# Value columns of a delta-rule mixer projected behind keys and queries, gates kept raw for two tiles, residual transposes issued later

## Chip, cores and metric

One core of one Trainium2 chip runs the whole kernel in one launch. The metric is device time in microseconds (us) of one execution; lower is better.

## What is computed

One decoder layer on x (512 tokens x 1024), all in float32. Cut to its order, the reference is:

```python
x = layer_norm(alpha * x + 0.5 * swiglu_ffn(x, ffn1_w13, ffn1_w2), ln1_g, ln1_b)
h = x @ w_in
gq, gk, gv, gz, ga, gb, dq, dk, dv = split(h)      # 512 columns each; ga, gb: 4
q, k, v = split(silu(causal_depthwise_conv(concat(gq, gk, gv), conv_w)))
q, k = l2_normalize(q), l2_normalize(k)            # 4 heads x 128
g, beta = -exp(a_log) * softplus(ga + dt_bias), sigmoid(gb)
y_a = rms_norm(gated_delta_rule(q, k, v, g, beta), norm_w) * silu(gz)
y_b = differential_attention(rotary(dq), rotary(dk), dv)   # 4 heads, two causal softmax maps each
x = layer_norm(alpha * x + concat(y_a, y_b) @ w_out, ln2_g, ln2_b)
ple = sigmoid(x @ ple_gate_w) * (p @ ple_proj_w)
x = layer_norm(alpha * x + 0.5 * swiglu_ffn(x, ffn2_w13, ffn2_w2) + ple, ln3_g, ln3_b)
```

## The kernel before, in words

Tokens stand in four tiles of 128 (index t). Every matrix product of the layer's weights is made of three TensorE products (`mm3`, lines 297 to 299): both operands are split into a high part that keeps the faster format and a low part that is the rest (`split`, lines 159 and 160: a ScalarE cast and a VectorE subtraction). The current activations lie transposed in XH and XL (channels on partitions), the residual itself in RES (tokens on partitions).

**Residual and transposes.** After each block the residual tile is normalised (`norm_natural`, line 302): statistics on VectorE, an inverse root on GpSimd (line 314), the first 768 columns on VectorE, the last 256 on ScalarE and GpSimd (lines 324 to 326). `norm_turn` (line 336) then transposes the tile on TensorE, eight 128x128 transposes into two PSUM banks (line 341), and splits it into XH and XL. The first FFN ends with products for tile after tile (`ffn`, lines 604 to 624); the turn of a tile follows the normalisation of the next one, and tile 3's turn stands in the first block of the mixer. The output projection (`out_gdn`, line 1288) does the same, and tile 3's turn stands among the gate products of the second FFN (line 787).

**The mixer.** First come attention values and decay inputs (`values_and_gates`), then `keys_queries`: eight columns, four heads of keys and four of queries. A column is 24 products over all 512 tokens from one weight unit; behind it `conv` applies the causal convolution (one ScalarE copy, line 895, three VectorE steps, line 897) and a Silu (line 899). `squares` turns a head to token order and sums its squares.

What follows is written by a small planner in the source. `weave` (line 97) holds lanes, each a generator that says what its last piece costs and how long its answer takes; the first lane that is ready issues next. In order of rank the lanes are: the end of the keys, four preparations of the delta rule (`gdn`, one for each tile), `diagonal` (a small triangular inverse with DMAs through DRAM), `chain` (the recurrence over four chunks, line 1197), sixteen attention heads (`attention`, line 1147: scores L1159, softmax, transposes L1172, products with values L1178; from `i` on a head waits for head `i - 2`), then `fill`, the big products that lie between the others, and last the two halves of the output projection. The chain opens when all `gdn` lanes, the values ("v") and the gates ("z") are said to be done; the attention half of the output projection opens when all heads and the gates are.

`fill` before: the attention keys, four token tiles (each 24 products in three cuts, a copy on ScalarE, line 1013, rotary on GpSimd, lines 906 to 910, and a turn of the tile, line 1002, held back until two cuts of the next tile are issued; the last key tile turns at once); the attention queries in the same way; four value columns of the delta rule with their convolution and `v_turn` (line 1049: four transposes and one VectorE product into VV, line 1052); and four gate tiles, each a Silu on ScalarE (line 1045) and a product with the norm weight on GpSimd (line 1046) into ZG, which lies on MP's first half.

The source gives the order by rank only. When the program is built, the instructions of each engine are put in order by rank and by the times at which their data are expected, so a piece can run before or behind its place in the source. `issue_after` ties a few by hand.

**Buffers.** PSUM has three tags: "a" with three banks (turns, preparation, chain), "b" with two (all big products, key and value turns), "c" with three (attention; two of them for the scores of one head from tile 2 on). "tb" in SBUF has two buffers (convolution, rotary, gates before). Weights come in units of 512 KB through SP's DMA queue into three raw buffers, are split into four pairs of buffers, and are fetched by `ahead`, once for each unit that is used up; a block over token tiles takes four units at once, a column takes one.

The steps that the prediction follows are in these lines:

```python
natural(t, cuts, gbt)                    # ffn, 618
...
if turn and t:                           # 623
    turn(t - 1)
...
if word == "k":                          # fill, 1018
    turn(*last)
    yield 0.5, 0
```

Of the kernel before, what the change touches and what calls it, by code (L numbers as in the profile page):

```python
# [11 lines left out]
AF = mybir.ActivationFunctionType  # L12
# [101 lines left out]
class Layer:  # L114
# [303 lines left out]
    def ffn(self, first_f, rec0, groups, plain, evac_first, ln, natural, turn):  # L418
# [191 lines left out]
        for t in range(NT):  # L610
            cuts = [0, 512, 1024]
            for j in range(t < 2, 2):
                end = not turn and t == NT - 1 and j == 1
                with self.behind([] if t else ended):
                    second(last, t, j, [(0, 256), (256, 512)] if end else [(0, 512)])
                if end:
                    cuts = [0, 512, 768, 1024]
            natural(t, cuts, gbt)
            if turn and t < 2:
                with self.behind(ended):  # L620
                    self.ahead()
                    self.ahead()
            if turn and t:
                turn(t - 1)


    def first_ffn(self):
# [114 lines left out]
    def second_ffn(self):  # L742
        tc, nc = self.tc, self.nc
        act, dve = nc.scalar, nc.vector
        with ExitStack() as zone:
            self.open_sums(zone)
            with ExitStack() as z2:
                pp = z2.enter_context(tc.tile_pool(name="ple", bufs=1))
                PH = pp.tile([P, 2, S], F32R, name="PH")
                PL = pp.tile([P, 2, S], F32R, name="PL")  # L750
                SG = pp.tile([P, NT, D], F32, name="SG")
                pr = [pp.tile([P, S], F32, name=f"pr{k}") for k in range(2)]
                hold = [pp.tile([P, 2, HALF], F32, name=f"hold{k}") for k in range(2)]
                for k in range(2):
                    nc.sync.dma_start(pr[k], self.pT[k])
                sums = self.combine(hold)

                def gate(t, j, wg):
                    tk = slice(t * P, (t + 1) * P)
                    pg = self.ps("b")  # L760
                    for k in range(KT):
                        c = (k % 2) * 512
                        self.mm3(pg, self.XH[:, k, tk], self.XL[:, k, tk], wg[k // 2][0][:, c:c + 512],
                                 wg[k // 2][1][:, c:c + 512], k == 0, k == KT - 1)
                        if t == NT - 1 and k % 2:
                            self.ahead()
                    act.activation(SG[:, t, j * 512:(j + 1) * 512], pg, AF.Sigmoid)

                def project(t, j):
                    tk = slice(t * P, (t + 1) * P)  # L770
                    pj = self.ps("c")
                    for k in range(2):
                        self.mm3(pj, PH[:, k, tk], PL[:, k, tk], wp[k][0][:, j * 512:(j + 1) * 512],
                                 wp[k][1][:, j * 512:(j + 1) * 512], k == 0, k == 1)
                    sg = SG[:, t, j * 512:(j + 1) * 512]
                    dve.tensor_tensor(sg, sg, pj, ALU.mult)
                    rj = self.RES[t][:, j * 512:(j + 1) * 512]
                    dve.scalar_tensor_tensor(rj, rj, ALPHA, sg, ALU.mult, ALU.add)

                wg = [self.take() for _ in range(4)]  # L780
                for t in range(NT):
                    if t == 1:
                        for k in range(2):
                            self.split(PH[:, k, :], PL[:, k, :], pr[k])
                        wp = [self.side(pp, f"wp{k}") for k in range(2)]
                    if t == 2:
                        self.norm_turn(NT - 1)
                    gate(t, 0, wg)
                for _ in range(2):
                    next(sums)  # L790
                wg = [self.take() for _ in range(4)]
                for t in range(NT):
                    gate(t, 1, wg)
                    project(t, 0)
                    for _ in range(2):
                        next(sums, None)
                for _ in sums:
                    pass
                for i in range(2):
                    self.split(*self.quarter(1, 0, 2 * i, 2), hold[i])  # L800
                for t in range(NT):
                    self.ahead()
                    project(t, 1)
                    self.ahead()

            def first(rj, pd, t, j):
                dve.scalar_tensor_tensor(rj, rj, 2.0, pd, ALU.mult, ALU.add)  # L807

            def store(t, lo, hi, rj):
                nc.sync.dma_start(self.out[t * P:(t + 1) * P, lo:hi], rj)  # L810

            def natural(t, cuts, gbt):
                self.norm_natural(t, 4.0 * LN_EPS, gbt, store, 768 if t < NT - 1 else D, cuts)

            self.open_ffn(zone)
            self.ffn(NF, NF - PLAIN, GROUPS2, None, first, G_LN3, natural, None)
# [6 lines left out]
    def mix_zone(self, zone):  # L823
# [88 lines left out]
        def values_and_gates():  # L912
            w = [self.take() for _ in range(4)]
            for t in range(NT):
                if t == 2:
                    self.norm_turn(NT - 1)
                tk = slice(t * P, (t + 1) * P)
                for i, (lo, hi) in enumerate(((0, DVA), (DVA, WIDE // 2))):
                    pq = ps("b")[:, 0:hi - lo]
# [38 lines left out]
        def keys_queries():  # L958
# [11 lines left out]
            for i in range(2):  # L970
                for h in range(H):
# [7 lines left out]
                    if i == 0 and h == 0:  # L979
                        gates()  # L980
                    elif i == 1 and h == 1:
                        gates_decay()
            yield
            squares(*held)
            pool.memset(UU, 0.0)
            dve.tensor_scalar(q1, SSK, RMS_EPS, None, ALU.add)
            dve.tensor_scalar(SSQ, SSQ, RMS_EPS, RMS_EPS * P, ALU.add, ALU.mult)
            dve.reciprocal(q2, q1)
            dve.tensor_tensor(CC, BETA, q2, ALU.mult)
            dve.tensor_tensor(CKR, CC, EG[:, 1], ALU.mult)  # L990
            dve.tensor_scalar(NEG_EG, EG[:, 0], -1.0, None, ALU.mult)
            for c in range(NC):
                pool.tensor_tensor(NRM[:, c], q1[:, c], phalf[:, 0:H], ALU.pow)

        def fill():
            for dst, word in ((DKT, "k"), (DQT, "q")):
                w = [self.take() for _ in range(4)]
                held = None

                def turn(t, d):  # L1000
                    pt = ps("b")
                    turn4(pt, v4(d))
                    dve.tensor_copy(dst[:, :, t * P:(t + 1) * P], v4(pt))
                    said.add((word, t))
                for t in range(NT):
                    pq = ps("b")
# [5 lines left out]
                    d = tb()  # L1012
                    act.copy(d, pq)
                    rotary(d, t)
                    held = (t, d)
                yield 0, 0
                last = held
                if word == "k":
                    turn(*last)
                    yield 0.5, 0  # L1020
            held = last
            for h in range(H):
                pq = ps("b")
                w = self.take()
                for i, (k0, k1) in enumerate(CUTS):
                    columns(pq, w, k0, k1)
                    yield 0.65 * (k1 - k0), 0
                    if i == 1 and h == 0:
                        turn(*held)
                    elif i == 1:  # L1030
                        self.v_turn(*held)
                vt = tb()
                conv(8 + h, pq, v4(vt))
                held = (h, vt)
            w = [self.take() for _ in range(4)]
            for t in range(NT):
                pq = ps("b")
                for i, (k0, k1) in enumerate(CUTS):
                    block(t, w, pq, k0, k1)
                    yield 0.65 * (k1 - k0), 0  # L1040
                    if t == 0 and i == 1:
                        self.v_turn(*held)
                        said.add("v")
                z = tb()
                act.activation(z, pq, AF.Silu)
                pool.tensor_tensor(ZG[:, t], v4(z), bc(VEC[:, V_NW:V_NW + P], 1, H), ALU.mult)
            said.add("z")

        def v_turn(h, vt):
            pt = ps("b")  # L1050
            turn4(pt, v4(vt))
            dve.tensor_tensor(VV[:, :, h, :], v4(pt), bc(NRM[:, :, h], 2, P), ALU.mult)

        self.v_turn = v_turn


        def lv4(l):
# [201 lines left out]
            yield 0.5, 1.0  # L1259


        def project_out(w, half, t):
            tk = slice(t * P, (t + 1) * P)
            for j in range(2):
                pd = ps("b")
                for k in range(4):
                    kk = k + 4 * (1 - half)
# [20 lines left out]
        def out_gdn():  # L1288
# [3 lines left out]
            for t in range(NT):  # L1292
                while ("mix", t) not in said:
                    yield 0, 0.5
                yield from project_out(w, 1, t)
                self.norm_natural(t, LN_EPS, gbt)
                if t:
                    self.norm_turn(t - 1)


        values_and_gates()
# [46 lines left out]
def layout(i):  # L1348
# [30 lines left out]
    wd = np.concatenate([dv[:, :256], ab, dv[:, 256:]], axis=1).reshape(4, 2, P, WIDE // 2).transpose(0, 2, 1, 3)  # L1379
    col_units(gk)  # L1380
    col_units(gq)
    nat_units(dk)
    nat_units(dq)
    col_units(gv)
    nat_units(gz)
    wo = i["w_out"][0]
    for k in (4, 5, 6, 7, 0, 1, 2, 3):
# [38 lines left out]
```

## Time and profile before

| | |
|---|---|
| median of 3 runs | 1098.65 us (1098.52 to 1100.03) |
| the profiled execution | 1099.23 us, its span 1097.4 us |
| TensorE (PE) busy | 1068.6 us, 97% of the span |
| VectorE (DVE) busy | 828.2 us, 75% |
| ScalarE (ACT) busy | 489.9 us, 45% |
| GpSimd (POOL) busy | 112.9 us, 10% |
| weights fetched | 127 units of 512 KB, 88 of 256 KB, 4 of 520 KB |

Times of the trace are us from the start of the span. The busy time of a matrix product overlaps that of the next one, so the time that a product costs is read from start to start. In a row of instructions the number in square brackets is the engine's idle time before it and what ended it. PEld is TensorE's load of the stationary operand.

### The profile page before, as it was taken

How to read it: one execution, taken by the hardware profiler on the slowest of the kernel's cores; microseconds unless marked ns; L12 is line 12 of the kernel's file. 1: busy time of each engine (PE TensorE's matmuls, PEld its weight loads, DVE VectorE, ACT ScalarE, POOL GpSimd, SP SyncE). 2: the span in 40 equal slices, each digit the busy share in tenths (PEclk: the TensorE clock that was granted, in tenths of full speed). 3: DMA queues.
4: the chain of work that ended last, by engine and by line, in shares of the span. 5: the costliest groups of instructions: out<-in, count | busy, mean ns of one | idle time of the engine just before them, and what ended most of it. 6: DMA issues, size and time to landing. Idle time of an engine off the chain costs nothing.

```text
span 1097.4 us, 17374 instructions
## 1 busy us (share of the span) xinstructions
PE 1068.6 (97%) x6627; PEld 939.8 (86%) x6627; DVE 828.2 (75%) x1446; ACT 489.9 (45%) x948; POOL 112.9 (10%) x175
## 2 busy tenths in 40 slices
PE   9999999999999989999999999999999999999996
PEld 7889898989897978778865887779899998999895
DVE  5989796979678366356665658889989696979568
ACT  5745353535333356324365533545544353535231
POOL 1100000000002202432112213100000000000003
PEclk9999999999999999999999999999999999999999
DMA  8633332433242042123210201524343332433212
GB/s 293 202 110 116 103 109 77 117 107 104 77 136 77 1 135 80 36 78 87 58 39 20 77 16 62 163 87 135 101 131 97 106 106 78 118 112 97 77 39 96
DMA packets 44275, 106.03 MB, mean 97 GB/s; under 512 B 10848, under 2 KB 12528, under 8 KB 44192
## 3 DMA queue, kind: packets, MB, share of 16 engines
q1 hardware_dynamic: 37968, 96.71, 29.0%
q0 software_dynamic: 1808, 6.04, 1.7%
q10 hardware_dynamic: 4416, 2.16, 0.7%
q8 instruction: 52, 0.85, 0.3%
q14 instruction: 31, 0.25, 0.1%
HBM read 102.41 MB, written 2.49 MB: 96 GB/s over the span
## 4 chain that ended last, share of the span: by engine, by line
PE 55%; DVE 5%; POOL 2%; DMA 2%; ACT 2%; issue 1%; DVEq 0%; SPq 0%; ACTq 0%; POOLq 0%
PE pb L297 9%; PE pb L298 9%; PE pb L299 9%; PE pc L298 4%; PE pc L299 4%; PE pc L297 4%; PE pa L299 3%; PE pa L298 3%; PE pa L297 3%; PE pc L1159 2%; DMA raw<-in_wa_dram 2%; DVE wl L160 2%; ACT wh L159 1%; PE pa L1092 1%; PE pc L1178 1%
## 5 line engine op out<-in xcount | busy, mean ns | idle before, releaser
L160 DVE TENSOR_TENSOR wl<-raw,wh 128x1024 fp32r<-128x1024 f32 (+3 forms) x137 | 144.2, 1058 | 37.6 <-ACT wh L159 36.4
L159 ACT CAST wh<-raw 128x1024 fp32r<-128x1024 f32 (+3 forms) x137 | 123.2, 906 | 96.7 <-PE pa L298 30.7
L297 PE MATMUL pb<-wh,hh 128*128 128x512 f32 (+1 forms) x356 | 138.3, 389 | 3.7 <-DVE RES L807 1.5
L298 PE MATMUL pb<-wl,hh 128*128 128x512 f32 (+1 forms) x356 | 138.1, 388 | 0.0
L299 PE MATMUL pb<-wh,hl 128*128 128x512 f32 (+1 forms) x356 | 137.8, 387 | 0.0
L229 ACT CAST th<-tr 128x512 fp32r<-128x512 f32 x160 | 98.7, 620 | 83.4 <-PE pc L298 48.2
L233 DVE TENSOR_TENSOR tl<-tr,th 128x512 fp32r<-128x512 f32 x160 | 109.7, 687 | 11.0 <-ACT th L229 10.2
L190 ACT CAST wh<-raw 128x512 fp32r<-128x512 f32 x88 | 54.6, 623 | 135.1 <-PE pb L299 90.8
L297 PE MATMUL pb<-wh,XH 128*128 128x512 f32 (+2 forms) x288 | 110.8, 385 | 2.2 <-ACT wh L159 0.6
L298 PE MATMUL pb<-wl,XH 128*128 128x512 f32 (+2 forms) x288 | 106.1, 369 | 1.0 <-DVE wl L160 0.9
L299 PE MATMUL pb<-wh,XL 128*128 128x512 f32 (+2 forms) x288 | 105.9, 368 | 0.0
L298 PE MATMUL pa<-XL,wh 128*128 128x256 f32 (+1 forms) x344 | 100.0, 291 | 0.2 <-DVE XL L160 0.2
L297 PE MATMUL pa<-XH,wh 128*128 128x256 f32 (+1 forms) x344 | 100.0, 291 | 0.2 <-ACT wh L159 0.2
L299 PE MATMUL pa<-XH,wl 128*128 128x256 f32 (+1 forms) x344 | 99.9, 290 | 0.0
L297 PE MATMUL pc<-XH,th 128*128 128x256 f32 x320 | 90.6, 283 | 0.0
L298 PE MATMUL pc<-XL,th 128*128 128x256 f32 x320 | 90.6, 283 | 0.0
L299 PE MATMUL pc<-XH,tl 128*128 128x256 f32 x320 | 90.6, 283 | 0.0
L490 DVE TENSOR_TENSOR RES<-RES,pb 128x512 f32<-128x512 f32 (+1 forms) x81 | 54.6, 677 | 45.1 <-PE pb L299 44.4
L191 DVE TENSOR_TENSOR wl<-raw,wh 128x512 fp32r<-128x512 f32 x88 | 60.2, 691 | 32.2 <-ACT wh L190 32.0
L297 PEld LDWEIGHTS pb<-wh,hh 128*128 128x128 f32 x356 | 66.9, 188 | 19.4 <-DVE RES L807 1.8
L299 PEld LDWEIGHTS pb<-wh,hl 128*128 128x128 f32 x356 | 66.9, 188 | 13.7
L298 PEld LDWEIGHTS pb<-wl,hh 128*128 128x128 f32 x356 | 66.9, 188 | 13.2 <-DVE wl L191 0.3
(303 smaller groups left out, 2639.8 us busy)
## 6 DMA issues: line engine op xcount, KB each, us to landing
raw<-in_wa_dram SPq DMA_DIRECT2D x127, 512.0 KB, 3.7
raw<-in_wb_dram SPq DMA_DIRECT2D x88, 256.0 KB, 2.7
raw<-in_wd_dram SPq DMA_DIRECT2D x4, 520.0 KB, 3.7
RES<-in_xn_dram POOLq DMA_DIRECT2D x4, 512.0 KB, 6.3
gb<-in_gb_dram POOLq DMA_DIRECT2D x8, 256.0 KB, 3.9
xr<-in_xT_dram ACTq DMA_DIRECT2D x7, 256.0 KB, 4.4
out_dram<-RES SPq DMA_DIRECT2D x5, 256.0 KB, 2.1
TT<-in_gb_dram POOLq DMA_DIRECT2D x4, 256.0 KB, 3.6
```

What stands on the lines that cost most here:

```text
L159: return (self.nc.scalar.copy(hi, src), self.nc.vector.tensor_tensor(lo, src, hi.bitcast(F32), ALU.subtract))
L160: self.nc.vector.tensor_tensor(lo, src, hi.bitcast(F32), ALU.subtract))
L190: nc.scalar.copy(hi, r)
L191: nc.vector.tensor_tensor(lo, r, hi.bitcast(F32), ALU.subtract)
L229: act.copy(h, t)
L233: dve.tensor_tensor(hl[1], t, hl[0].bitcast(F32), ALU.subtract)
L297: pe.matmul(o, wh, xh, start=first, stop=False)
L298: pe.matmul(o, wh, xl, start=False, stop=False)
L299: pe.matmul(o, wl, xh, start=False, stop=last)
L490: dve.tensor_tensor(rj, rj, pd, ALU.add)
L1092: pe.matmul(pt[:, h * P:(h + 1) * P], MP[:, 0, c, h, :], TT[:, c, h, :], start=True, stop=True)
L1159: pe.matmul(sc[m], DQT[r, h, t * P:(t + 1) * P], DKT[r, h, 0:n], start=True, stop=False)
```

## The change

Five things. The four value columns leave `fill` and stand in `keys_queries` behind the queries, one column at a time without a cut; the norm factors NRM that `v_turn` needs are worked out at the first of them. The last key tile's turn is held back into the first query tile, and the last query tile's into the first gate tile. A gate tile is copied raw into ZG by ScalarE, and after every second one a Silu and the GpSimd product run over both. In the first FFN the turns of tiles 0 and 1 are issued behind the second half of tile 2's products and the first half of tile 3's, those of tiles 2 and 3 ahead of the second and third block of `values_and_gates`; at the output projection likewise, with tiles 2 and 3 turned behind the first and second gate block. The units of gv stand ahead of dk's in DRAM, as they are now used.

```diff
@@ ffn
                 if end:
                     cuts = [0, 512, 768, 1024]
+                if turn and (t, j) in ((2, 1), (3, 0)):
+                    turn(t - 2)
             natural(t, cuts, gbt)
...
-            if turn and t:
-                turn(t - 1)
@@ second_ffn
-                    if t == 2:
-                        self.norm_turn(NT - 1)
                     gate(t, 0, wg)
+                    if t < 2:
+                        self.norm_turn(NT - 2 + t)
@@ values_and_gates
-                if t == 2:
-                    self.norm_turn(NT - 1)
+                if t in (1, 2):
+                    self.norm_turn(NT - 3 + t)
@@ keys_queries
+            for h in range(H):
+                pq = ps("b")
+                columns(pq, self.take(), 0, KT)
+                if h == 0:
+                    squares(*held)
+                    dve.tensor_scalar(q1, SSK, RMS_EPS, None, ALU.add)
+                    for c in range(NC):
+                        pool.tensor_tensor(NRM[:, c], q1[:, c], phalf[:, 0:H], ALU.pow)
+                else:
+                    v_turn(*held)
+                vt = tb()
+                conv(8 + h, pq, v4(vt))
+                held = (h, vt)
             yield
-            squares(*held)
+            v_turn(*held)
+            said.add("v")
             pool.memset(UU, 0.0)
-            dve.tensor_scalar(q1, SSK, RMS_EPS, None, ALU.add)
...
-            for c in range(NC):
-                pool.tensor_tensor(NRM[:, c], q1[:, c], phalf[:, 0:H], ALU.pow)
@@ fill
-            for dst, word in ((DKT, "k"), (DQT, "q")):
+            held = None
+            for word in "kq":
                 w = [self.take() for _ in range(4)]
-                held = None
...
-                    held = (t, d)
+                    held = (word, t, d)
                 yield 0, 0
-                last = held
-                if word == "k":
-                    turn(*last)
-                    yield 0.5, 0
-            held = last
-            for h in range(H):
-                pq = ps("b")
-                w = self.take()
-                for i, (k0, k1) in enumerate(CUTS):
-                    columns(pq, w, k0, k1)
-                    yield 0.65 * (k1 - k0), 0
-                    if i == 1 and h == 0:
-                        turn(*held)
-                    elif i == 1:
-                        self.v_turn(*held)
-                vt = tb()
-                conv(8 + h, pq, v4(vt))
-                held = (h, vt)
             w = [self.take() for _ in range(4)]
...
                     if t == 0 and i == 1:
-                        self.v_turn(*held)
-                        said.add("v")
-                z = tb()
-                act.activation(z, pq, AF.Silu)
-                pool.tensor_tensor(ZG[:, t], v4(z), bc(VEC[:, V_NW:V_NW + P], 1, H), ALU.mult)
+                        turn(*held)
+                act.copy(ZG[:, t], v4(pq))
+                if t % 2:
+                    z = ZG[:, t - 1:t + 1].rearrange("p t h b -> p (t h) b")
+                    act.activation(z, z, AF.Silu)
+                    pool.tensor_tensor(z, z, bc(VEC[:, V_NW:V_NW + P], 1, 2 * H), ALU.mult)
@@ out_gdn
-                yield from project_out(w, 1, t)
+                for j in range(2):
+                    yield from project_out(w, 1, t, (j,))
+                    if j == 0 and t > 1:
+                        self.norm_turn(t - 2)
                 self.norm_natural(t, LN_EPS, gbt)
-                if t:
-                    self.norm_turn(t - 1)
@@ layout
     col_units(gk)
     col_units(gq)
+    col_units(gv)
     nat_units(dk)
     nat_units(dq)
-    col_units(gv)
     nat_units(gz)
```

## Rows read from the trace of the kernel before

**Rows 1.** The profile page, part 1: TensorE's busy time, share, instructions.

```profile
PE 1068.6 (97%) x6627; PEld 939.8 (86%) x6627; DVE 828.2 (75%) x1446; ACT 489.9 (45%) x948; POOL 112.9 (10%) x175
```

**Rows 2.** Waits of TensorE, whole span: us in total, times, longest us.

```profile
PE pa L341 <- POOL RES L326: 3.6, 4, 1.3
```

**Rows 3.** TensorE's timeline at the end of the first FFN: start us, us, engine.

```profile
346.76 0.82 PE L341 MATMUL pa<-CST,RES 128*128 128x128 f32 x6
...
349.05 0.48 PE L299 MATMUL pb<-wh,hl 128*128 128x512 f32 x1
...
352.35 1.17 PE L341 MATMUL pa<-CST,RES 128*128 128x128 f32 x8
353.27 0.48 PE L298 MATMUL pb<-wl,hh 128*128 128x512 f32 x1
...
357.25 0.82 PE L341 MATMUL pa<-CST,RES 128*128 128x128 f32 x6
...
359.51 0.37 PE L297 MATMUL pb<-wh,XH 128*128 128x264 f32 x1
...
365.32 0.27 PE L341 MATMUL pa<-CST,RES 128*128 128x128 f32 x1
```

**Rows 4.** The timeline of all engines there: GpSimd's last piece of tile 0.

```profile
348.08 0.72 POOL L326 TENSOR_TENSOR RES<-RES,gb 128x256 f32<-128x256 f32 x1
```

**Rows 5.** TensorE's timeline behind the output projection: turns of tiles 0 and 2.

```profile
670.34 0.81 PE L341 MATMUL pa<-CST,RES 128*128 128x128 f32 x6
...
671.90 0.48 PE L297 MATMUL pb<-wh,XH 128*128 128x512 f32 x1
...
683.87 0.82 PE L341 MATMUL pa<-CST,RES 128*128 128x128 f32 x6
...
685.40 0.48 PE L297 MATMUL pb<-wh,XH 128*128 128x512 f32 x1
686.29 0.50 PE L298 MATMUL pb<-wl,XH 128*128 128x512 f32 x1 [0.41 <-DVE wl L160]
```

**Rows 6.** TensorE's timeline at the end of the attention keys.

```profile
468.62 1.89 PE L1074 MATMUL pa<-KQ 128*128 128x256 f32 x8
472.09 0.66 PE L871 MATMUL pb<-CST,tb 128*128 128x128 f32 x4 [1.59 <-POOL tb L910]
```

**Rows 7.** The timeline at one of the two waits for a value turn.

```profile
558.64 0.60 PE L871 MATMUL pb<-CST,tb 128*128 128x128 f32 x4
...
559.32 0.38 PE L1220 MATMUL pa<-VV,UU 128*128 128x128 f32 x2
...
560.03 0.50 PE L297 MATMUL pb<-XH,wh 128*128 128x512 f32 x1 [0.33 <-DVE VV L1052]
```

**Rows 8.** ScalarE's groups, 380 to 700 us: count | busy us, mean ns | idle.

```profile
L899 ACT ACT_TABLE_LOAD x6 | 7.7, 1283 | 6.2 <-DVE tb L897 6.2
L1164 ACT ACT_TABLE_LOAD x5 | 6.4, 1283 | 4.3 <-DVE amx L1162 4.3
```

**Rows 9.** Timelines of GpSimd, VectorE and TensorE at one gate tile.

```profile
582.06 1.27 POOL L1046 TENSOR_TENSOR MP<-tb,VEC 128x512 f32<-128x512 f32 x1 [5.39 <-ACT tb L1045]
...
582.09 1.25 DVE L1184 SCALAR_TENSOR_TENSOR aso<-aso 128x1 f32<-128x1 f32 x1
...
584.42 0.94 PE L1178 MATMUL pc<-DV,tt 128*128 128x128 f32 x6 [0.56 <-DVE DQT L1186]
```

**Rows 10.** Windows: stretch, length, busy us of PE, PEld, DVE, ACT, POOL; clock.

```profile
541.00:615.00 74.00, 71.95 (x338) 48.84 (x337) 45.19 (x105) 46.19 (x95) 12.02 (x22) 1.00 0.12 35
615.00:656.20 41.20, 40.35 (x259) 35.89 (x257) 24.11 (x50) 17.59 (x53) 7.80 (x7) 1.00 0.15 41
```

**Rows 11.** TensorE's groups: two of 541 to 615, one of 615 to 656.2.

```profile
L297 PE MATMUL pb<-wh,XH 128*128 128x512 f32 x32 | 13.4, 420 | 0.3 <-DVE VV L1052 0.3
...
L297 PE MATMUL pb<-XH,wh 128*128 128x512 f32 x24 | 10.0, 418 | 0.3 <-DVE VV L1052 0.3
...
L297 PE MATMUL pb<-wh,XH 128*128 128x512 f32 x33 | 13.7, 415 | 0.0
```

More of the change, by code (lines that the diff above doesn't have):

```diff
@@ L991, in keys_queries, with turn @@
             dve.tensor_scalar(NEG_EG, EG[:, 0], -1.0, None, ALU.mult)
-            for c in range(NC):
-                pool.tensor_tensor(NRM[:, c], q1[:, c], phalf[:, 0:H], ALU.pow)
         def fill():
-            for dst, word in ((DKT, "k"), (DQT, "q")):
+            held = None
+            for word in "kq":
                 w = [self.take() for _ in range(4)]
-                held = None
-                def turn(t, d):
+                def turn(word, t, d):
                     pt = ps("b")
                     turn4(pt, v4(d))
-                    dve.tensor_copy(dst[:, :, t * P:(t + 1) * P], v4(pt))
+                    dve.tensor_copy((DKT if word == "k" else DQT)[:, :, t * P:(t + 1) * P], v4(pt))
                     said.add((word, t))
@@ L1052, in v_turn @@
             dve.tensor_tensor(VV[:, :, h, :], v4(pt), bc(NRM[:, :, h], 2, P), ALU.mult)
-        self.v_turn = v_turn
         def lv4(l):
@@ L1259, in chain, with project_out @@
             yield 0.5, 1.0
-        def project_out(w, half, t):
+        def project_out(w, half, t, js=(0, 1)):
             tk = slice(t * P, (t + 1) * P)
-            for j in range(2):
+            for j in js:
                 pd = ps("b")
```

## The prediction

> **What bounds the kernel now.** I read four views in this order. The table of engines [rows 1] says that TensorE is busy 97% of the span, so all that an edit of order can win is what TensorE waits, plus the time in which a product is held up inside a busy stretch. The list of waits of TensorE, longest first, names who ended them; its longest line is the transposes of the normed residual, which wait four times for GpSimd's last piece of the normalisation [rows 2]. The timeline of TensorE around each such place gives the size of a wait from start to start of its products, which is firmer than the busy column. The windows of the two mixer stretches [rows 10] show what covers the latency of the attention heads and of the chain, the point where this change can lose. The granted clock is 1.00 in both, so no term below is a change of clock.
>
> The profiled execution took 1099.23 us (a span of 1097.4 and 1.8 around it), 0.6 us above the median of the runs shown, 1098.65. I sum against 1099.2 and take the same difference off the median. A difference under 0.2%, 2.2 us, is about what a measurement of this kernel can't tell from no change.
>
> **The change part by part.**
>
> *Transposes behind the first FFN.* An undisturbed turn (eight transposes) takes 353.27 - 352.35 = 0.92 us. The turn of tile 0 takes 349.05 - 346.76 = 2.29 and that of tile 2 359.51 - 357.25 = 2.26 [rows 3], so 1.37 + 1.34 = 2.7 us are waits. By the program, the turn of tile 0 now stands behind both products of tile 2's halves. In the trace it ran 7 products before the end of those. Fourteen products lie between 349.05 and 352.35, 0.23 us each, so it starts 1.6 us later, at 348.4. Its first six transposes last until 349.1, and GpSimd's last piece is ready at 348.08 + 0.72 = 348.8 [rows 4]: no wait is left. The turn of tile 2 moves behind the whole first block of values (359.51 to 365.32, 5.8 us), long after its data. What needs it, values of tile 2, comes one block later still. I take **-2.7 us**; the bounds are -2.7 and 0.
>
> *Transposes behind the output projection.* The first turn takes 671.90 - 670.34 = 1.56, 0.64 too much. The third takes 685.40 - 683.87 = 1.53, but the gate block behind it waits for the low half of its weights anyway: its second product starts at 686.29, 0.66 later than it would [rows 5]. Today the transposes cover part of that wait; taken away, the wait grows by what they used, up to 0.92, and the transposes still come later. So -0.64 at one place against a loss of about that at the other: **0**, bounds -1.2 and +0.9.
>
> *The last key turn.* It is held over into the first query tile, behind two thirds of that block. Today TensorE stands 1.59 us for GpSimd's rotary at the end of the keys [rows 6]; counted from the end of the eight products before it, it is 1.7. Eighteen query products now lie between, 4 us of cover for a wait of 1.7. The attention heads that need all keys come much later. **-1.7**, bounds -1.7 and 0. The last query turn moves from the first value column to the first gate tile in the same way: 0.
>
> *Value columns out of the fill, behind the queries.* Ninety-six products of 0.23 us, 21.8 us, move and cost the same. In the fill, the transposes of a finished value head make the next column wait for their PSUM bank; this was seen twice, 0.33 us each [rows 7], and goes: **-0.7**. In the new place the same turn stands three times between two columns, with both banks of that tag in use: from the last transpose of 558.64 to the next column at 560.03 the trace has about 1.0 us that is not column work. Three of them are +3.0 if nothing comes between; the lower bound is 0, because the delta-rule preparation, several microseconds of products on other banks, depends on nothing that is still missing. That such a thing is drawn forward is seen in the same rows: a product of the chain (L1220), which the program has behind the end of the gates, ran at 559.32. I take **+1.0**, nearer the lower end. ScalarE's table loads between Silu and Exp, 11 in these two lines at 1.28 us [rows 8], fall by about 7, 9 us of ScalarE; TensorE hardly waits for that engine there, so 0 (bound -1).
>
> *Gate weights.* The four units of the gates are now fetched and split during one query tile instead of one with each value column. A block that takes four fresh units at its start waited 0.66 in [rows 5]; heads can stand in between, so **+0.5**, bounds 0 and +1.4.
>
> *Raw gates.* Four Silu and four GpSimd products over 512 columns become four copies, and two of each over 1024. On ScalarE that is some more work under cover. On GpSimd a product of 1.27 us becomes one of about 2.5. While one ran, a VectorE instruction on a single column, begun 0.03 us later, took 1.25 us, and TensorE waited 0.56 for what hung on it [rows 9]. Taken with the next part. The Trainium skill (SBUF — State Buffer, section Terms, the line on the shared port pair) says that VectorE and GpSimd hold that pair exclusively for a full instruction, the loser blocking fully; the rows agree so far. By that rule alone one wait would grow by some 1.3 us and the sum with it; by the row, in which less than half of the block reached TensorE, by about 0.6.
>
> *What covers the heads and the chain.* Between 541 and 615 us, 56 x 3 = 168 big products (38 us) of values and gates alternate with the heads' 36 us; between 615 and 656, 33 x 3 products of the output projection (22 us) fill the chain, and TensorE is idle 0.85 us in 41 [rows 10, 11]. After the change the value products are gone from the first stretch (72 of the 168), and most of the first gate tile comes ahead of it: some 18 us of fill are left, the gates end before half of the heads' work is done, and the chain starts beside them. Heads and chain then cover each other, the output projection behind both. About 18 us of heads stand against 22 us of gaps, so idle time of 4 us is the plain reading, up to 8 if both wait together, 0 if output projection blocks are drawn forward as L1220 was. A gain is possible too, up to 2 us, from a lighter VectorE and ScalarE. With the GpSimd block I take **+0.6**, bounds -2 and +8.
>
> **Sum**: -2.7 - 1.7 - 0.7 + 1.0 + 0.5 + 0.6 = -3.0 us. 1099.2 - 3.0 = 1096.2 in a profiled run like this one; against the median **1095.6 us**.
>
> **Rivals.**
> *Chain and heads uncovered (slower).* The place is the stretch from the end of the gates to the end of the last head. For it: 21.8 us of cover leave, and the heads have started no earlier in their own order; each needs many small steps on three engines. Against it: the forward draw of rows 7. At 7 us of idle time instead of 0.6 the sum is +3.4, 1102.0 us. It decides from 0.6 + 3.0 + 2.2 = 5.8 us on. Chance 0.23.
> *Waits exchanged.* The value turns cost their full 3.0 and the late stretch 3: -5.1 + 3.0 + 0.5 + 3 = +1.4, 1100.0 us. For it: the column stage has only two banks of this tag. Against it: free preparation work. Chance 0.15.
> *The change doesn't do what it says.* The order on TensorE isn't the program's: the turn of tile 0 stands behind 48 products of its group in the program and ran behind 65. If the turns are again put where their data seem ready, 2.7 stays and the sum is -0.3, 1098.4 us. Against it: a place later in the program is a lower rank. Chance 0.10.
>
> **How the numbers follow.** My forecast, several waits removed and the cover kept, has 0.52; it is faster by over 0.2%. The exchange and the unchanged order give the same time, 0.25. The uncovered stretch gives slower, 0.23. All gains with no cost are -5.1 - 2 - 1 = -8.1, 1090.5; for the top I take the slow rival with another microsecond, 1103. The forecast's own range is 1091 to 1096.4.
>
> **What would show it.** Right: the list of waits has the residual's transposes for GpSimd at under 1 us; the turn of the last keys waits for nothing; no wait for the value turns in the stretch of the heads; table loads down by about seven. Wrong: TensorE idle over 4 us between the end of the gates and the output projection, with waits on the heads' or the chain's VectorE and ScalarE steps; columns that wait a microsecond each for the value turns; a gate block behind the output projection that waits over 1.5 us for its weights.

## The result and the profile after

The changed kernel takes **1106.17 us** (median of 11 runs, 1102.45 to 1112.11) beside 1098.65 for the kernel before: ratio 1.0071, 95% interval 1.0051 to 1.0092, so slower by 0.7%. I had forecast 1095.6 and a range up to 1103.0. The execution with the profile took 1102.71 us, a span of 1100.9.

In the table of engines TensorE still stands at 97%, which says nothing of where the time went:

```profile
PE 1070.4 (97%) x6627; PEld 942.6 (86%) x6627; DVE 826.3 (75%) x1446; ACT 486.5 (44%) x947; POOL 111.9 (10%) x173
```

The list of waits of TensorE in the changed kernel (us in total, times, longest) does:

```profile
PE pc L1170 <- ACT tt L1166: 3.8, 2, 3.5
PE pa L1197 <- ACT ST L1225: 2.2, 1, 2.2
...
PE pc L1170 <- DVE DQT L1178: 1.3, 1, 1.3
PE pb L297 <- ACT AB L928: 1.3, 1, 1.3
PE pb L871 <- POOL tb L910: 1.0, 1, 1.0
PE pb L297 <- DVE tb L897: 0.8, 2, 0.6
...
PE pa L341 <- POOL RES L326: 0.4, 1, 0.4
```

The same places in the kernel before, where L1178 is the heads' product that is L1170 now:

```profile
PE pb L297 <- DVE tb L897: 1.8, 2, 1.2
...
PE pb L871 <- POOL tb L910: 1.6, 1, 1.6
...
PE pc L1178 <- DVE DQT L1186: 0.6, 1, 0.6
...
PE pb L297 <- ACT AB L928: 0.4, 1, 0.4
```

The residual's transposes, 3.6 us before [rows 2], now wait 0.4 us. At the head of the list stand two waits that were not there, both for ScalarE: those of the heads' products with values (L1170) and of the chain (L1197). The same heads' products also wait longer for VectorE, 1.3 us for 0.6, and so does the values block behind the first FFN for ScalarE (L928), 1.3 us for 0.4.

Windows of the changed kernel (us, then busy us of PE, PEld, DVE, ACT, POOL with instruction counts, granted clock, DMA share, GB/s):

```profile
340.00:420.00 80.00, 76.30 (x445) 65.62 (x443) 50.68 (x96) 33.23 (x83) 19.63 (x23) 1.00 0.24 73
420.00:541.00 121.00, 119.64 (x592) 94.75 (x591) 67.96 (x153) 52.13 (x120) 34.22 (x61) 1.00 0.26 72
541.00:615.00 74.00, 68.27 (x422) 52.43 (x420) 43.30 (x109) 37.07 (x100) 17.36 (x26) 1.00 0.14 44
615.00:656.20 41.20, 37.04 (x211) 29.16 (x212) 22.41 (x59) 15.96 (x54) 4.78 (x9) 1.00 0.00 1
541.00:660.00 119.00, 109.11 (x648) 84.74 (x647) 66.87 (x169) 53.03 (x153) 22.13 (x35) 1.00 0.09 27
```

The same for the kernel before, where [rows 10] don't have it:

```profile
340.00:420.00 80.00, 74.33 (x434) 63.61 (x434) 48.36 (x94) 32.94 (x82) 16.85 (x20) 1.00 0.21 67
420.00:541.00 121.00, 119.11 (x663) 96.45 (x662) 69.52 (x166) 45.09 (x121) 39.35 (x72) 1.00 0.25 68
541.00:660.00 119.00, 115.56 (x606) 86.81 (x605) 72.36 (x158) 65.25 (x153) 19.82 (x28) 1.00 0.15 44
```

Idle time is window less PE. From 340 to 541 us it falls from 7.6 to 5.1. The residual's transposes and the last key turn have their share in that; 1.0 us of it is the wait for the convolution (L897), which falls as much in `key_only` below, where nothing at that place is changed. In the two mixer windows it rises from 2.05 + 0.85 [rows 10] to 5.73 + 4.16, by 7.0 us. The DMA share of 0.00 in the second is the output projection not fetching weights. In the timeline no product of L297 to L299 runs between 590.3 and 639. The heads begin 20 us later, behind the moved columns (first scores at 504.2 instead of 484.1); the last product of the last head starts at 637.4 instead of 612.2, and the program opens the output projection only behind all heads.

What such a wait is made of, in the timeline of the changed kernel (lines of TensorE and ScalarE, not all of them):

```profile
595.48 1.06 ACT L1039 ACTIVATE MP<-MP 128x1024 f32<-128x1024 f32 x1
595.77 0.66 PE L1222 MATMUL pa<-ta,KD 128*128 128x128 f32 x4
596.84 1.28 ACT L1156 ACT_TABLE_LOAD   x1 [0.29 <-DVE amx L1154]
597.17 0.49 PE L1164 MATMUL pc<-CST,tt 128*128 128x128 f32 x3
598.70 0.55 ACT L1156 ACTIVATE pc<-pc,amx 128x384 f32<-128x384 f32 x1
599.26 0.58 ACT L1225 COPY ST<-pa 128x512 f32<-128x512 f32 x1
599.89 0.94 PE L1197 MATMUL pa<-ST,KQ 128*128 128x128 f32 x6 [2.23 <-ACT ST L1225]
...
630.06 0.60 PE L1164 MATMUL pc<-CST,tt 128*128 128x128 f32 x4
631.35 0.67 ACT L1156 ACTIVATE tt<-pc,amx 128x512 f32<-128x512 f32 x1
632.01 0.65 ACT L1156 ACTIVATE pc<-pc,amx 128x512 f32<-128x512 f32 x1
633.26 0.30 ACT L1239 ACTIVATE VV<-KQ 128x128 f32<-128x128 f32 x1
633.55 0.57 ACT L1166 COPY tt<-pc 128x512 f32<-128x512 f32 x1
634.17 1.16 PE L1170 MATMUL pc<-DV,tt 128*128 128x128 f32 x8 [3.51 <-ACT tt L1166]
```

The transposes end at 630.66, but ScalarE copies them out at 633.55 only: in its queue the softmax of the next head (L1156) and the chain's squares (L1239) stand ahead. In the same way the chain's state is in PSUM at 596.43 and copied at 599.26, behind a table load and a head's softmax. (The table load is the way back from the Silu of a gate pair, L1039. In `tile_gates` below, which has no pairs, this wait isn't in the list, but another one for ScalarE of 2.1 us is.) In these two places the heads and the chain don't cover each other; they queue for one ScalarE.

### The profile page after: what moved, and what is told of

It reads as the page before. It is cut to its first block, busy times and chain, and to the rows that moved or that the text cites. A ratio compares the mean times of both kernels' runs of the same rounds, so it can differ in the third digit from the quotient of the medians.

```text
span 1100.9 us, 17363 instructions
## 1 busy us (share of the span) xinstructions
PE 1070.4 (97%) x6627; PEld 942.6 (86%) x6627; DVE 826.3 (75%) x1446; ACT 486.5 (44%) x947; POOL 111.9 (10%) x173
## 4 chain that ended last, share of the span: by engine, by line
PE 51%; DVE 7%; ACT 3%; DMA 3%; POOL 2%; issue 2%; DVEq 0%; SPq 0%; ACTq 0%; POOLq 0%
PE pb L297 8%; PE pb L298 8%; PE pb L299 8%; PE pc L297 4%; PE pc L299 4%; PE pc L298 4%; PE pa L298 3%; PE pa L299 3%; PE pa L297 3%; DMA raw<-in_wa_dram 2%; PE pc L1151 2%; DVE wl L160 1%; ACT wh L159 1%; PE pa L1084 1%; DVE tb L897 1%
## 5 line engine op out<-in xcount | busy, mean ns | idle before, releaser
L160 DVE TENSOR_TENSOR wl<-raw,wh 128x1024 fp32r<-128x1024 f32 (+3 forms) x137 | 142.2, 1044 | 38.8 <-ACT wh L159 37.8
L297 PE MATMUL pb<-wh,hh 128*128 128x512 f32 (+1 forms) x356 | 138.1, 389 | 2.4 <-ACT wh L159 1.1
L299 PE MATMUL pb<-wh,hl 128*128 128x512 f32 (+1 forms) x356 | 137.8, 387 | 0.0
L297 PE MATMUL pb<-wh,XH 128*128 128x512 f32 (+2 forms) x288 | 109.6, 381 | 2.7 <-ACT AB L928 1.3
L299 PE MATMUL pb<-wh,XL 128*128 128x512 f32 (+2 forms) x288 | 106.0, 368 | 0.0
L297 PE MATMUL pa<-XH,wh 128*128 128x256 f32 (+1 forms) x344 | 100.3, 292 | 0.0
L299 PE MATMUL pa<-XH,wl 128*128 128x256 f32 (+1 forms) x344 | 100.1, 291 | 0.0
L297 PE MATMUL pc<-XH,th 128*128 128x256 f32 x320 | 90.6, 283 | 0.0
L299 PE MATMUL pc<-XH,tl 128*128 128x256 f32 x320 | 90.6, 283 | 0.0
L297 PEld LDWEIGHTS pb<-wh,hh 128*128 128x128 f32 x356 | 66.9, 188 | 17.3 <-ACT wh L159 1.5
L299 PEld LDWEIGHTS pb<-wh,hl 128*128 128x128 f32 x356 | 66.9, 188 | 13.7
```

The lines of the kernel that those rows point to most:

```text
L160: self.nc.vector.tensor_tensor(lo, src, hi.bitcast(F32), ALU.subtract))
L297: pe.matmul(o, wh, xh, start=first, stop=False)
L299: pe.matmul(o, wl, xh, start=False, stop=last)
```

## The experiments

The kernel before ran beside each group; its medians were 1096.8 to 1097.5 us. The diffs are against the kernel named, cut to the core.

**One part alone, and one part undone.** `v_only` is before with nothing but the columns moved; `v_back` is the changed kernel with only the columns back in the fill; `turns_only` and `key_only` are before with one kind of turn moved.

```diff
 v_only (before)                         v_back is its reverse, on the changed kernel
+            for h in range(H):
+                pq = ps("b")
+                columns(pq, self.take(), 0, KT)
...
 key_only (before)
-                if word == "k":
-                    turn(*last)
-                    yield 0.5, 0
...
 turns_only (before)
+                if turn and (t, j) in ((2, 1), (3, 0)):
+                    turn(t - 2)
...
-            if turn and t:
-                turn(t - 1)
...
```

> The kernel before with one part of the change: the value columns behind keys and queries; turns, gates and the last key turn as before. Theory (cover): the loss comes from this part, since heads and chain then run without big products beside them. Expected 1105 to 1110 us, as far above the changed kernel as the changed kernel's other parts save (2 to 4 us), a spread between runs of several us, and a mean granted clock under 0.997 in the slower runs. Rival (gates): the loss comes from the gate pairs, whose long GpSimd products hold VectorE up; then 1097 to 1099.5 us with the small spread of the kernel before.

> The changed kernel with the value columns back in the fill, all else as changed. Cover: 1094 to 1097 us (the turns give 2.7, the last key turn some 1 to 2), spread of the kernel before, granted clock 0.998 in all runs, TensorE idle under 4 us between the end of the delta-rule levels and the output projection. Gates: above 1100 us.

> The kernel before with the residual turns alone moved. Both theories: 1095.5 to 1097 us (the waits of 1.4 and 1.3 us behind the first FFN gone, nothing net at the output projection). Second rival (exchange): a new wait behind the turns takes the gain, 1098 to 1099.5 us.

> The kernel before with nothing but the last key and query turn of a tile held back behind the next block. If the trace of the changed kernel reads rightly (2.7 us less issue time around the key turn), 1095 to 1096.5 us. If holding the turn costs something later (the query's products are late for the heads), 1098 us or more.

Measured: `v_only` 1104.52 us, ratio 1.0058 (1.0044 to 1.0072); `v_back` 1094.66, 0.9969 (0.9959 to 0.9980); `turns_only` 1095.00, 0.9976 (0.9967 to 0.9985); `key_only` 1094.01, 0.9972 (0.9963 to 0.9981). The loss is in the place of the columns; all that is left without it is a gain. The changed kernel and `v_back` differ by that place alone, and by 1.0071 / 0.9969 = 1.010, some 11 us. Moved alone, from the kernel before, the columns cost 7.0 us: the price depends on what else is changed.

**How much cover.** `v_half` leaves two of the four column groups in the fill.

```diff
 v_half (changed kernel)
-            for h in range(H):
+            for h in range(2):
...
+            for h in range(2, H):
...
```

> The changed kernel with two of the four groups of value columns projected behind the queries, and two left in the fill beside the heads. The cover theory: the time lies between the kernel with all columns back in the fill (2.8 us below before) and the changed kernel (8 to 10 us above before), that is 1097 to 1103 us, the last head's output ends near 624 us, between 611 and 637 to 643, and the granted clock falls for less time than in the changed kernel. If what costs is that columns leave the fill at all (their place behind the queries), half of them cost half in the stretch before 541 us, and not between 590 and 640.

Measured 1098.12 us, 1.0019 (1.0010 to 1.0028): between the two, as cover would have it. The last product of its last head starts at 626.4, also between (610.9 in `v_back`). The window 541 to 660 has 6.8 us idle, against 9.9 in the changed kernel and 4.0 in `v_back`; from 420 to 541 it has 0.8 us against 0.7 in `v_back`, so half of the columns cost nothing behind the queries that would show (first `v_half`, then `v_back`):

```profile
541.00:660.00 119.00, 112.19 (x608) 83.67 (x606) 68.56 (x168) 59.01 (x157) 20.45 (x33) 1.00 0.10 32
```

```profile
541.00:660.00 119.00, 115.00 (x607) 87.42 (x607) 72.58 (x159) 65.95 (x159) 18.02 (x28) 1.00 0.15 45
```

**Other cover: a miss.** `out_early` opens the attention half of the output projection tile by tile, to put big products beside the heads.

```diff
 out_early (changed kernel)
+                while not {("attn", t, h) for h in range(H)} <= said:
+                    yield 0, 0.5
...
-        need_out = {("attn",) + th for th in heads} | {"z"}
+        need_out = {"z"}
...
```

> The changed kernel with the attention half of the output projection opened tile by tile, as soon as a tile's heads and the gates are done, instead of after all heads. Cover: its 192 big products go between heads and chain, TensorE's idle time in the stretch from 555 to 640 us falls from 9.9 us to under 4, granted clock 0.997 or more in all runs, 1094 to 1098 us. Gates or exchange: the time stays at 1102 to 1106 us, since nothing of either is touched.

Measured 1107.2 us, 1.0084 (1.0070 to 1.0098): no help. The first of its blocks ran at 600.2, between the heads, and the last head's last product moved from 637.4 to 656.7. By the program the blocks' turns share the heads' PSUM tag; that this held the heads up is argued, not shown. The idle time, 4.8 us from 600 to 640 and none from 640 to 660 in the changed kernel, moved with the heads:

```profile
600.00:640.00 40.00, 38.30 (x234) 30.16 (x234) 24.81 (x69) 17.09 (x65) 7.84 (x12) 1.00 0.00 1
640.00:660.00 20.00, 14.70 (x68) 10.75 (x67) 9.37 (x27) 7.51 (x25) 2.50 (x5) 0.91 0.00 0
```

**Relief of the heads with the columns still moved.** `heads_first` ranks the heads ahead of the chain, `heads_b` gives them the gates' PSUM banks once the gates are done, `heads_both` does both.

```diff
 heads_first (changed kernel): the line of chain() below the heads' lanes
-        lanes.append(Lane(chain(), lambda: need_chain <= said))
...
+        lanes.append(Lane(chain(), lambda: need_chain <= said))
 heads_b (changed kernel)
-            pt = ps("c")
+            spare = "b" if "z" in said else "c"
+            pt = ps(spare)
...
-            po = ps("c")
+            po = ps(spare)
```

> The changed kernel with the heads ranked ahead of the chain. Heads: the last head ends some 5 us earlier and the chain later, in part under the output projection, which covers it as in the kernel before: 1098 to 1103 us. Cover: heads without the chain beside them wait more, the chain follows, and the sum is the same or worse: 1102 to 1112 us.

> The changed kernel with the transposes and the output of each head issued after the gates in the two banks of tag b, which stand empty there, instead of sharing the three banks of tag c with the scores. Theory (heads): the sixteen heads are a series of about 130 us whose pace their banks and steps set, and the change starts them 20 us later; so with more banks the last head ends 6 us or more ahead of 637 us and the kernel takes 1096 to 1101 us. Rival (cover): only big products beside heads and chain help; then the last head ends where it did and the time stays at 1102 to 1110 us.

> The changed kernel with the heads ahead of the chain of the first output tile, and with their transposes and outputs in the gates' PSUM banks once the gates are done. If the two reliefs add (each took 5 to 8 us off the changed kernel), 1096 to 1099 us. If both only remove the same waits, 1099.5 to 1101 us as each alone. Idle of TensorE between 541 and 660 us: 4 us or less in the first case, about 6.5 in the second.

Measured: `heads_first` 1100.88 us, 1.0042 (1.0027 to 1.0056); `heads_b` 1100.56, 1.0034 (1.0022 to 1.0047), though the last head's last product came only 0.7 us earlier (636.7), not the 6 us expected; `heads_both` 1095.44, 0.9990 (0.9981 to 0.9998). Against the changed kernel beside them (`after_again` below, 1.0088) the two reliefs add, and with the columns still moved they give back 9 us against the first measurement of the changed kernel, 11 against the second. In the list of waits of `heads_both` neither the 3.5 nor the 2.2 us for ScalarE is left. Its window has 4.6 us idle:

```profile
541.00:660.00 119.00, 114.45 (x679) 89.00 (x678) 71.01 (x174) 56.72 (x158) 22.14 (x35) 1.00 0.11 34
```

**The control.** `back_heads` has both reliefs and the columns in the fill (the diffs of `v_back` and `heads_both` together).

> The changed kernel with the value columns back in the fill (2.8 to 3.4 us below before) and with both reliefs of the heads (their rank ahead of the chain, the gates' PSUM banks). With the columns moved, the two reliefs took 12 us off. If what they relieve is only there because the heads stand alone, they are worth little beside a fill that covers them: 1092.5 to 1095 us, at most 2 us from the same kernel without them. If they are simply better for the heads, whatever stands beside them, 1087 us or less, and the columns would cost what they cost in either form.

Measured 1094.14 us, 0.9979 (0.9969 to 0.9988), against 0.9969 without the reliefs: worth nothing there. So what they relieve exists only when the heads stand without cover. Read the other way, the place of the columns costs 11 us without the reliefs and about 1 with them (0.9990 against 0.9979).

**The changed kernel once more**, without an edit, as `after_again`.

> The changed kernel again, for comparison on this chip. 1102 to 1110 us; runs with a lower mean granted clock are the longer ones, by about 11 us for each hundredth, and a profile with a clock of 0.996 or less shows the half clock inside the stretch of heads and chain.

Measured 1108.21 us, 1.0088 (1.0065 to 1.0111). Its profiled execution took 1109.12 us, 6.4 more than the first one. The list of waits from 541 to 660 is nearly the same, and so is the idle time, 10.1 us against 9.9. The granted clock is not:

```profile
541.00:660.00 119.00, 108.92 (x617) 85.43 (x616) 67.17 (x166) 53.10 (x153) 22.13 (x35) 0.93 0.09 27
...
560.00:575.00 15.00, 13.56 (x67) 9.15 (x66) 7.83 (x23) 5.98 (x15) 4.69 (x7) 1.00 0.06 19
575.00:579.00 4.00, 4.00 (x12) 2.39 (x12) 1.08 (x5) 2.89 (x7) 0.74 (x2) 0.58 0.00 0
...
596.00:599.50 3.50, 3.50 (x17) 3.20 (x16) 3.07 (x3) 0.98 (x1) 2.35 (x1) 0.51 0.10 39
...
637.00:644.00 7.00, 5.91 (x27) 5.69 (x28) 3.46 (x11) 2.71 (x10) 1.72 (x3) 0.51 0.01 2
```

0.5 is the lower of the two levels, 1.2 GHz. The program got 617 products done in the window instead of 648, and the last product of the last head starts at 643.4 instead of 637.4.

**Gates.** `tile_gates` and `both_tile` are the changed kernel and `heads_both` with the gates made one tile at a time again. `turns_key` is before with both kinds of turns: `v_back` without the paired gates.

```diff
 tile_gates, both_tile (changed kernel, heads_both)
-                act.copy(ZG[:, t], v4(pq))
-                if t % 2:
...
+                z = tb()
+                act.activation(z, pq, AF.Silu)
...
```

> The changed kernel with the gates tile by tile as before (Silu and a 512-column GpSimd product for each), the columns still moved. If the pairs cost nothing, 1102 to 1110 us, as the changed kernel on this chip within 2 us; the earlier runs add up to 1102 (1104.5 with the columns moved alone, less 2.6 for the turns), so a pair cost of 2 to 4 us, by GpSimd's longer products, would show here as 1101 to 1103 us against 1105 to 1107.

> The kernel before with the residual turns ahead of the last block and with the last key and query turn held back; value columns stay in the fill and gates are made tile by tile. Alone the turns took 2.6 us and the key turn 3.1 us off. If they add, 1091 to 1092 us, and the gate pairs of the changed kernel cost the 2 to 3 us by which the changed kernel with its columns back in the fill (ratio 0.9969) misses that sum. If they do not add, because the heads and the chain give part of an earlier start back, 1094 to 1095 us, and the gate pairs cost nothing here either.

> The changed kernel with both reliefs of the heads (1095.4 us with them) and with the gates made one token tile at a time again. If a paired gate holds up the heads and the chain wherever it falls, as it seems to beside a full fill (3 us between the kernel with both turns and the changed kernel with its columns back), 1092 to 1093.5 us. If it costs something only beside a full fill, as the changed kernel with gates by tile suggests (no difference to the changed kernel), 1095 to 1096 us. What then still separates it from 1090.7 us, the kernel with both turns and the columns in the fill, is the price of the moved columns once the heads are relieved.

Measured: `tile_gates` 1105.81 us, 1.0082 (1.0069 to 1.0095); `both_tile` 1097.59, 1.0002 (0.9990 to 1.0014), no better than with pairs; `turns_key` **1090.74, 0.9942** (0.9930 to 0.9955), the fastest of all and faster than both kernels, where the ratios of the two turns multiply to 0.9948. So beside a full fill the pairs cost about 3 us (0.9969 against 0.9942), and with the columns moved nothing that shows. From 541 to 660 us `turns_key` has 2.1 us idle, `v_back` 4.0, though the profiled execution of `turns_key` was its slowest (1093.42):

```profile
541.00:660.00 119.00, 116.86 (x612) 87.90 (x611) 72.97 (x166) 65.62 (x157) 19.42 (x29) 1.00 0.15 49
```

The timeline of `v_back` has the place, the last pair beside the chain:

```profile
611.95 1.28 ACT L1042 ACT_TABLE_LOAD   x1
613.24 1.06 ACT L1042 ACTIVATE MP<-MP 128x1024 f32<-128x1024 f32 x1
...
614.37 2.36 POOL L1043 TENSOR_TENSOR MP<-MP,VEC 128x1024 f32<-128x1024 f32 x1 [3.90 <-ACT MP L1042]
...
614.77 1.98 DVE L1181 SCALAR_TENSOR_TENSOR aso<-aso 128x1 f32<-128x1 f32 x1
...
615.08 0.50 PE L297 MATMUL pb<-wh,XH 128*128 128x512 f32 x1 [0.94 <-ACT XH L159]
...
617.41 0.66 PE L871 MATMUL pc<-CST,DQT 128*128 128x128 f32 x4 [1.15 <-DVE XL L160]
```

In `turns_key` the same VectorE step is L1179, and it falls behind the gate's product:

```profile
609.62 1.28 POOL L1041 TENSOR_TENSOR MP<-tb,VEC 128x512 f32<-128x512 f32 x1
...
612.99 0.53 DVE L1179 SCALAR_TENSOR_TENSOR aso<-aso 128x1 f32<-128x1 f32 x1
```

In `v_back` a step on one column stands 1.98 us beside the 2.36 us product; the split of the next operand (L160) is queued behind it and TensorE waits 1.15. Ahead of that, 2.3 us of table load and Silu hold up a cast, another 0.94. The Trainium skill (SBUF — State Buffer, section Terms) has the loser of the shared port pair block for the other's whole instruction; the row agrees: the step ends with the product, at 616.7. The 0.53 us in `turns_key` end in the same way, at 613.5, with a GpSimd step of the chain (L1205, 612.46 + 1.04).

**Turns with the columns moved.** `v_turns` is `v_only` with the residual turns of `turns_only`.

> The kernel before with the value columns projected behind keys and queries, and with the two residual turns ahead of their last block; gates are made one token tile at a time and the last key and query turn are done at once. If the parts add, it takes the time of the value columns alone (7.0 us above before in the run of the first call) less the 2.5 us of the turns: 1101 to 1102.5 us beside a before of 1097.2 to 1097.5. If the residual turns are worth nothing once the heads stand alone, 1104 us or more. Neither the held key turn nor the paired gates are in it, so a time of 1105 us or more would clear both of them of what is left of the loss.

Measured 1104.46 us, 1.0067 (1.0049 to 1.0085): the turns' 2.5 us don't show. In its profile the heads start 2.8 us earlier than in `v_only` (507.0 against 509.8) and the span is shorter (1101.4 against 1106.3), but the medians are alike, and the runs spread over 7 us. What swallows the gain was not settled.

## Why the prediction failed

**Failed step: "What covers the heads and the chain".** The step gave the right mechanism and named 4 us of idle time as "the plain reading", but its +0.6 is the share of the GpSimd block alone: the idle time itself went into the sum at nothing, trusting that (in its words) "Heads and chain then cover each other" and that output projection blocks would be drawn forward as one product of the chain had been [rows 7]. None was drawn forward: the program opens that projection behind all heads, and the last head came 25 us later. Where it was forced, in `out_early`, it did not help. And heads and chain held each other up at ScalarE. In place of the 0.6 the two mixer windows lost 7.0 us. The slow rival was priced at that: 7 us of idle time and +3.4. The profiled execution at full clock came out at +3.5 (1102.71 against 1099.23). That the two agree so closely is in part luck: the gain before 541 us was 2.5 us, less than the 3.4 us forecast there, and another 1 us net lies outside these windows, where the sum has no term for it. `v_half`, `heads_both` and `back_heads` show the cause, each from another side.

**Failed too: "no term below is a change of clock".** The rows of before have 1.00 in both mixer windows, and I took that as given. Between the two profiled executions of the changed kernel, with nearly the same waits, the clock is the difference I can see for 6.4 us. The median lies 3.5 us above the profiled run and past the range. Most of that goes with the clock: the five runs with a mean of 0.994 or less took 1107.34 us and more, the six others 1106.17 and less. It isn't all, since the median run itself has 0.997. Why the clock fell in one execution and not in the other is open.

**Residual turns: -2.7 and 0 forecast, -2.6 measured** (`turns_only`). The wait for GpSimd fell from 3.6 to 0.4 us in the changed kernel; the wait at L928 grew by 0.9 us, with the turns alone too, and was not foreseen. In the traces the wait at L897 fell by 1.0 us besides; no run shows that the turns did this, and without it they would have fallen short of the forecast.

**Last key turn: -1.7 forecast, -3.1 measured** (`key_only`). Its own wait fell from 1.6 to 0.4 us. The rest is not at the turn: idle time falls from 5.7 to 4.8 us from 340 to 420, mostly at L897, and from 3.4 to 1.9 from 541 to 660; the cause was not sought. In the changed kernel 1.0 us of the key turn's wait stays.

**Value columns behind the queries: +1.0 forecast, about +0.7 found, at another place.** The window 420 to 541 has 1.4 us idle, and 0.7 in `v_back`, where the columns are in the fill. One value turn waits 0.3 us; the rest is the last key turn, which waits longer when the columns stand ahead of it, 1.0 us instead of 0.4 when it is held back, and 2.6 instead of 1.6 when it is not:

```profile
PE pb L871 <- POOL tb L910: 2.6, 1, 2.6
```

That is `v_only`; `v_turns` has the same line. So the columns cost little where they went to, but some 11 us where they had been. The two waits for a value turn's bank (-0.7) are gone from the list; what that saved can't be told beside the loss. Table loads fell from 20 to 17, not by seven. For the gate weights (+0.5) the list of waits has nothing from 420 to 660 us.

**Raw gates: right place, wrong weight.** Forecast as one longer GpSimd product, part of the +0.6; beside a full fill they cost 3 us, more than half of the turns' gain. The rows of `v_back` have ScalarE's share, 0.94 us, on top of GpSimd's 1.15. That they cost nothing more in the changed kernel because the stretch was waiting already is my reading; no run shows why.

**The rival "waits exchanged"** falls: the value turns wait 0.3 us, not 3.0. **"The change doesn't do what it says"** falls too: the residual's waits went, and the last key turn's in part.

## What to carry to other kernels

Work that costs the same wherever it stands isn't free to move: before moving big products out of a stretch, count what is left there to cover the step-by-step work, and look up what opens the next big products. If they open only behind that same work, the products taken out come back as idle time. Try each part of such a change alone; here two of them were worth 0.6% together and the other two ate it.

## What the hardware showed that I had not expected

In the thin stretch the granted clock fell to 1.2 GHz four times, for 17 us in all, in one execution and not at all in the other of the same program. TensorE had been busy 13.56 of 15 us before the first fall, with no idle time longer than 1.26 us, and 13.90 where it stayed at full clock:

```profile
560.00:575.00 15.00, 13.90 (x68) 9.20 (x66) 7.48 (x23) 6.18 (x17) 4.95 (x7) 1.00 0.08 19
```

The 11 runs go from 1102.45 us at a mean clock of 0.997 to 1112.11 at 0.988. A full fill doesn't rule it out: the profiled execution of `key_only`, with 1.9 us idle from 541 to 660, fell to the lower level once, at 586. And `heads_both`, at 1.00 throughout that window in its profiled execution, spread over 5 us, its two slowest runs at a mean clock of 0.994. The Trainium skill (TensorE: Matmul & The Clock Gate, section A second HAM failure mode: psum-queue depth-cycling) tells of a kernel whose TensorE idles briefly between groups of products, often enough for the clock to go back and forth between its two levels. The first fall of the changed kernel agrees with that, and the two executions show that such gaps alone don't fix it from one execution to the next.
